# Seven half-size products for the five dense projections, with operands built in place, and down-weight sums formed where they are used

## The chip, the cores and the metric

The kernel runs on one core of a Trainium2 chip. The engines are TensorE (PE in the profile, PEld for its weight loads), VectorE (DVE), ScalarE (ACT), GpSimd (POOL) and SyncE (SP), whose queue issues all of this kernel's DMAs. The metric is the device time of one execution in microseconds (us). A measurement of this kernel tells differences from about 0.2% on.

## The reference

One decoder block over 1024 tokens of width 1024, in float32. Two sequence mixers (an SSD branch and a gated-linear-attention branch) are merged, then comes attention over 256 memory tokens and a gated FFN of width 2816, each with RMSNorm and a residual add:

```python
y_ssd = ssd_mixer(z, xBC, dt_raw, ...)
y_gla = gla_mixer(q, k, v, r, a1, ...)
merged = sigmoid(g_ssd) * (y_ssd @ w_up_ssd) + sigmoid(g_gla) * (y_gla @ w_up_gla)
h = h + merged @ w_o
q = rmsnorm(h) @ w_xq                 # 4 heads of 256
h = h + softmax(q k^T / 16) v @ w_xo  # k, v from the memory tokens
g, u = split(rmsnorm(h) @ w_ffn_in, 2)
h = h + (silu(g) * u) @ w_ffn_out
return rmsnorm(h)
```

The five matrices w_up_ssd, w_up_gla, w_o, w_xq and w_xo are 1024x1024 each; they are what the change is about, beside w_ffn_out.

## The kernel before

Activations are held transposed (features on partitions, tokens along the row) in quadrants: feature half i, token half j. Every float32 matrix product is made of three passes on parts of reduced precision: an operand is **split** into a high part, a copy on ACT (line 220), and a low part, a subtraction on DVE or POOL (line 74 records all calls of these two engines; the function `either` chooses one of them while the program is traced, by a running estimate of when each would be done). High x high, high x low and low x high are summed in PSUM.

The input projection, FFN-in and FFN-down use a scheme of seven products (Strassen's, in Winograd's form) in place of eight: with operand quadrants A (weights) and X, the products named B11, B21, T1, B22, T2, T3 and T4 use A11, A12, A21, A22 and sums of them (T1: A21+A22; T2: that less A11; B22: A12 less that; T3: A11-A21), and the same for X. The class `Operands` builds the X side, `Unit` the weight side for 256 columns, and `group` steps through the products, in the order SPACED for one unit and PAIRED for two.

The five dense projections before the change use plain products instead: `dense` walks over 8 blocks of 128 output features and 2 token halves, and each of these 16 outputs takes 24 matmuls of 128x128 by 128x512 into one PSUM bank (tiles `acc`), with weights split by `Left` (tiles `wd`, from `raw`) and inputs held split whole (tiles `hl`). After each output `post` evacuates the bank: sigmoid gates and a multiply for the two merges (the first one's result goes to DRAM, `ysg_d`, and comes back), a residual add, a store and a square for the statistics (`ssum`) of w_o and w_xo, a split for w_xq. Beside the first four of them runs `presum`: it loads w_ffn_out, forms the four sums that FFN-down's seven products need (tiles `sa` and `raw`) and stores them in DRAM (`down_d`).

Attention (`Att`) comes between w_xq and w_xo, head by head. FFN-in runs 11 pairs of units (gate and up), FFN-down (`stream`, `piece`, `fevac`) walks through 7 products of 11 rows of blocks, two at a time (a piece, 24 matmuls), and loads each piece's left and right operand from DRAM (tiles `fr`), splits them (tiles `fs`) and multiplies.

The order of instructions is set by a scheduler that takes the traced instructions by priority (`ahead` raises one); the engines run their queues in that order. Buffers come from pools: `op` 14 buffers of 8 KB per partition, `aux` 4, `m` 4; PSUM has 4 banks `acc` and 4 banks `bank`.

Of the kernel before, what the change touches and what calls it, by code (L numbers as in the profile page):

```python
# [9 lines left out]
F32 = mybir.dt.float32  # L10
# [6 lines left out]
P = 128  # L17
# [23 lines left out]
PAIRED = ("B11", "T1", "B21", "T2", "T3", "B22", "T4")  # L41
# [38 lines left out]
def block_kernel(ctx: ExitStack, tc: tile.TileContext, t: dict, out: bass.AP):  # L80
# [39 lines left out]
    down_d = dram("down_d", 4 * D_FF // 2, HALF)  # L120
# [105 lines left out]
    class Operands:  # L226
# [44 lines left out]
    class Unit:  # L271
# [18 lines left out]
        def left(s, name):  # L290
# [3 lines left out]
            if name == "T1":  # L294
                s.S, s.two = sums[s.side].tile([P, s.kh, P], F32, name="sa", tag="sa", bufs=2), False
# [9 lines left out]
            return {"B11": A11, "B21": A12, "B22": A12, "T3": A21, "T4": A22}.get(name, s.S)  # L305
# [83 lines left out]
    def group(units, B, then=(), nxt=None, frm=6, products=7):  # L389
# [6 lines left out]
        for n, name in enumerate((PAIRED if many > 1 else SPACED)[:products]):  # L396
# [692 lines left out]
    ysg_d = dram("ysg_d", D, TOK)  # L1089

    def load_blocks(src, row0, n, key="m"):
        r = []
        for k in range(n // 2):
            b = slot(key, name="in")
            SP.dma_start(b, src[row0 + 2 * k * P:row0 + (2 * k + 2) * P, :].rearrange("(i p) s -> p i s", p=P))
            r.append(b)
# [511 lines left out]
```

## Time and profile before

| what | value |
| --- | --- |
| three runs, us | 2013.74, 2016.06 (median), 2016.79 |
| profiled execution: time, us | 2017.15 |
| profiled execution: span, us | 2015.4 |
| mean granted clock of TensorE | 0.991 |
| instructions in the profile | 26277 |
| DMA traffic | 309.60 MB, mean 154 GB/s |

The span runs from the first to the last instruction that the profiler saw; the profiled execution's time is 1.75 us longer and lies 1.09 us above the median. The profile's lines have a source line, an engine, an operation, the tiles written and read, the shape, a count, the busy time and the mean time of one.

### The profile page before, as it was taken

To read this page: it belongs to the slowest core of one execution; us is meant where nothing else is said; L and a number is where in the kernel's file an instruction comes from. 1 tells how busy PE (TensorE), PEld (TensorE's weight loads), DVE (VectorE), ACT (ScalarE), POOL (GpSimd) and SP (SyncE) were. 2 spreads that over 40 slices of the span, in tenths; PEclk is the share of its full clock that TensorE was granted. 3 is DMA by queue.
4 is the path that set the end of the run, shared out by engine and by line. 5 is a ranking of instruction groups with operands and counts; after the bars stand their busy time and mean duration, and the time that the engine had idled before them with its cause. 6 is when DMAs were issued, how large, how long until landed. Compare 5 with 4: busy or idle time off the path is not lost.

```text
span 2015.4 us, 26277 instructions
## 1 busy us (share of the span) xinstructions
PE 1937.9 (96%) x9740; PEld 1617.2 (80%) x9740; DVE 1250.2 (62%) x1763; ACT 897.0 (45%) x1581; POOL 716.9 (36%) x524
## 2 busy tenths in 40 slices
PE   7798899999999999999999999998999999999998
PEld 6797687777777878888878888876888888888887
DVE  5855649879876655633444328566767667674465
ACT  7433844466553555542333226453343343354243
POOL 2612435556554212232134310244454554430002
PEclk9899999999999999999999999999999999999999
DMA  8441332255643755685775520432323323276463
GB/s 286 147 126 62 120 105 106 104 185 184 202 152 115 224 169 157 221 301 193 247 243 188 177 84 22 136 121 89 104 79 110 126 78 105 89 256 228 149 227 127
DMA packets 243365, 309.60 MB, mean 154 GB/s; under 512 B 14986, under 2 KB 162676, under 8 KB 243236
## 3 DMA queue, kind: packets, MB, share of 16 engines
q1 hardware_dynamic: 243236, 307.92, 45.6%
q8 instruction: 76, 1.25, 0.3%
q14 instruction: 53, 0.43, 0.1%
HBM read 211.07 MB, written 96.80 MB: 153 GB/s over the span
## 4 chain that ended last, share of the span: by engine, by line
PE 66%; DVE 8%; DMA 8%; POOL 6%; issue 6%; ACT 4%; SPq 2%; POOLq 0%; ACTq 0%; DVEq 0%
PE acc L52 58%; PE bank L52 7%; POOL raw L74 2%; DVE wlo L74 2%; DVE cv L74 1%; DMA raw<-in_w_in_dram 1%; PE bank L56 1%; POOL sa L74 1%; POOL y L74 1%; ACT whi L220 1%; DVE o L74 1%; DMA sr<-sr_d 1%; DMA vraw<-in_w_in_dram 1%; DMA ga<-yg_d 1%; ACT e L881 1%
## 5 line engine op out<-in xcount | busy, mean ns | idle before, releaser
L52 PE MATMUL acc<-hl,wd 128*128 128x512 f32 x1920 | 439.9, 390 | 1.7 <-DVE hl L74 0.8
L52 PEld LDWEIGHTS acc<-hl,wd 128*128 128x128 f32 x1920 | 360.1, 188 | 77.0 <-DVE hl L74 1.2
L74 DVE TENSOR_TENSOR wlo<-raw,whi 128x512 fp32r<-128x512 f32 x268 | 244.5, 915 | 129.4 <-ACT whi L220 128.7
L220 ACT ACTIVATE whi<-raw 128x512 fp32r<-128x512 f32 x272 | 169.8, 628 | 247.3 <-PE acc L52 194.7
L74 DVE TENSOR_TENSOR o<-acc,o 128x512 f32<-128x512 f32 (+1 forms) x160 | 107.2, 674 | 88.5 <-PE acc L52 85.9
L52 PE MATMUL acc<-fs 128*128 128x512 f32 (+1 forms) x792 | 156.2, 356 | 0.6 <-ACT o L1505 0.5
L74 POOL TENSOR_TENSOR sa<-raw 128x512 f32<-128x512 f32 x56 | 82.6, 1474 | 206.8 <-DMA raw<-in_w_ffn_out_dram 95.2
L52 PEld LDWEIGHTS acc<-fs 128*128 128x128 f32 x792 | 130.7, 189 | 21.6 <-ACT o L1505 0.9
L74 POOL TENSOR_TENSOR sa<-sa,raw 128x512 f32<-128x512 f32 x48 | 73.0, 1521 | 172.0 <-DVE wlo L74 172.0
L220 ACT ACTIVATE fs<-fr 128x1024 fp32r<-128x1024 f32 (+1 forms) x84 | 80.1, 984 | 110.2 <-PE acc L52 43.4
L74 DVE TENSOR_TENSOR fs<-fr,fs 128x1024 fp32r<-128x1024 f32 (+1 forms) x84 | 98.0, 1198 | 39.7 <-ACT fs L220 39.4
L74 POOL TENSOR_TENSOR raw<-raw,sa 128x512 f32<-128x512 f32 x48 | 76.8, 1600 | 91.6 <-DVE wlo L74 91.4
L220 ACT ACTIVATE whi<-sa 128x512 fp32r<-128x512 f32 x96 | 60.4, 629 | 109.2 <-PE acc L52 67.1
L74 POOL TENSOR_TENSOR raw<-raw 128x512 f32<-128x512 f32 x68 | 103.6, 1529 | 7.6 <-DVE sa L74 4.8
L74 DVE TENSOR_TENSOR wlo<-sa,whi 128x512 fp32r<-128x512 f32 x96 | 79.1, 824 | 37.7 <-ACT whi L220 37.5
L74 DVE TENSOR_TENSOR wd<-raw,wd 128x1024 fp32r<-128x1024 f32 x40 | 51.8, 1302 | 65.2 <-ACT wd L220 57.5
L74 DVE TENSOR_TENSOR ga<-acc,ga 128x512 f32<-128x512 f32 x64 | 43.8, 687 | 69.7 <-PE acc L52 56.0
L74 POOL TENSOR_TENSOR o<-o 128x512 f32<-128x512 f32 x39 | 63.4, 1629 | 59.4 <-DVE o L74 34.9
L52 PE MATMUL acc<-B22h,whi 128*128 128x512 f32 x192 | 77.4, 403 | 7.0 <-ACT whi L220 7.0
L52 PE MATMUL acc<-T2h,whi 128*128 128x512 f32 x192 | 77.4, 403 | 3.1 <-ACT whi L220 2.8
L52 PE MATMUL acc<-T2h,wlo 128*128 128x512 f32 x192 | 76.5, 399 | 3.8 <-DVE wlo L74 3.8
L52 PE MATMUL acc<-T1h,whi 128*128 128x512 f32 x192 | 76.2, 397 | 3.8 <-ACT whi L220 3.8
(370 smaller groups left out, 4832.9 us busy)
## 6 DMA issues: line engine op xcount, KB each, us to landing
raw<-in_w_in_dram SPq DMA_DIRECT2D x26, 1024.0 KB, 6.2
raw<-in_w_ffn_in_dram SPq DMA_DIRECT2D x22, 1024.0 KB, 7.6
act_d<-o SPq DMA_DIRECT2D x77, 256.0 KB, 2.0
fr<-act_d SPq DMA_DIRECT2D x35, 512.0 KB, 4.9
raw<-in_w_ffn_out_dram SPq DMA_DIRECT2D x11, 1024.0 KB, 6.9
fr<-down_d SPq DMA_DIRECT2D x20, 512.0 KB, 4.9
down_d<-raw SPq DMA_DIRECT2D x33, 256.0 KB, 2.7
raw<-in_w_xkv_dram SPq DMA_DIRECT2D x8, 1024.0 KB, 10.9
```

Of the source, the lines that this page charges most:

```text
L52: return s.e.matmul(o, x, y, **kw)
L56: return s.e.transpose(o, x, i)
L74: return f(*a, **kw)
L220: ACT.activation(hi, src, AF.Copy)
L881: ACT.activation(s.e[:, h], s.csb[:, h], AF.Relu, bias=cs[:, s.i0 + h:s.i0 + h + 1], scale=-1.0)
```

## The change

The five dense projections become products of seven as well (class `Product`), with whole quadrants of 512x512x512 each, every one in two halves of the inner dimension (24 matmuls each, 128x512). A `Grid` holds the four quadrants of an input as float32 tiles (`X`). `build(t)` forms the operands of half product t: it sums the weights in place in `raw`, splits them, sums the X quadrants in place, splits them, and puts the parts in two tiles `lr`; the loop builds two half products ahead (DEPTH). The products come in the order LATE. Each keeps four PSUM banks, one per 128 output features; `first` takes a bank's value into the output quadrant, `last` adds the bank to it and applies gate, residual or split. Gates and residuals are loaded by `early` into the rings `whi` and `wlo`. The first merge's result stays on the chip (`y_ys`), so `ysg_d` goes. Attention's heads come in another order, and two half products of w_xo are put into its end.

`presum` and `down_d` go. FFN-down's `stream` loads the raw quadrants of w_ffn_out (two for T1, B22 and T3, none for T2) and forms the sums there, with the running sum kept in tiles `rs`. `Unit.left` writes B22's left operand into the sum's tile instead of over A12, and two units are stepped in the order LATE instead of PAIRED.

```diff
-PAIRED = ("B11", "T1", "B21", "T2", "T3", "B22", "T4")
+LATE = ("B11", "T1", "T2", "B22", "T3", "B21", "T4")
@@ Unit.left
-            elif name in ("B22", "T2"):
-                if not s.two:
-                    sub(e, s.S, s.S, A11)
-                    s.two = True
-                if name == "B22":
-                    sub(either(A11, 2.0), A12, A12, s.S)
+            elif name == "T2":
+                sub(e, s.S, s.S, A11)
+            elif name == "B22":
+                sub(e, s.S, A12, s.S)
...
+    class Product:
+        RAW = {"B11": ((0, 0),), "T1": ((1, 0), (1, 1)), "B22": ((0, 1),), "T4": ((1, 1),)}
...
+        def left(s, name, ks):
+            r = lambda i, j: s.raw[i, j][:, ks]
+            e = lambda ap: either(ap, 2.0)
+            if name == "T1":
+                if ks.start == 0:
+                    s.S = s.raw[1, 1]
+                S = s.S[:, ks]
+                add(e(S), S, r(1, 0), S)
+                sub(e(S), r(1, 0), r(0, 0), r(1, 0))
+                return S
+            if name == "T2":
+                S = s.S[:, ks]
+                sub(e(S), S, S, r(0, 0))
+                return S
+            if name == "B22":
+                S = s.S[:, ks]
+                sub(e(S), S, r(0, 1), S)
+                return S
+            return r(*{"B11": (0, 0), "T3": (1, 0), "B21": (0, 1), "T4": (1, 1)}[name])
+
+        def build(s, t):
...
+            x = [slot("op", (P, 2, 2, HALF), F32R, name="lr") for _ in range(2)]
+            with ahead():
+                src = s.left(name, ks)
+                split(src, x[0][:, 0], x[0][:, 1], either(src))
+                if comb:
+                    comb[0](either(src, 1.0), q(of), q(comb[1]), q(comb[2]))
+                split(q(of), x[1][:, 0], x[1][:, 1], either(src))
+            s.hl[t] = x
+
+        def mm(s, t):
...
+            for k in range(2):
+                for u in range(4):
+                    for m, (a, b) in enumerate(((0, 0), (0, 1), (1, 0))):
+                        PE.matmul(s.p[u], w[:, a, k, u * P:(u + 1) * P], x[:, b, k],
...
+    DEPTH = 2
+    for t_ in range(4 * 14):
+        st, n = divmod(t_, 14)
+        nxt, m = divmod(t_ + DEPTH, 14)
+        if nxt < 4:
+            prods[nxt].build(m)
...
+        prods[st].mm(n)
...
@@ attention
+        if n >= 5:
+            if n < 9:
+                xo.build(n - 5)
...
+            if n in (7, 8):
+                xo.mm(n - 7)
@@ FFN-down, stream
-    LEFT = {"B11": (0, 0), "B21": (0, 1), "T1": 0, "B22": 3, "T2": 1, "T3": 2, "T4": (1, 1)}
+    LEFT = {"B11": ((0, 0),), "B21": ((0, 1),), "T1": ((1, 0), (1, 1)), "B22": ((0, 0), (0, 1)), "T2": (),
+            "T3": ((0, 0), (1, 0)), "T4": ((1, 1),)}
...
+                if name == "T1":
+                    add(e(), S, other, main)
+                elif name == "B22":
+                    sub(e(), S, S, other)
+                    sub(e(), main, main, S)
+                elif name == "T3":
+                    sub(e(), main, other, main)
+                split(S if name in ("T1", "T2") else main, x[0][:, 0], x[0][:, 1])
+                split(r[0][:, 1], x[1][:, 0], x[1][:, 1])
```

What this moves on the engines is shown at three places. First POOL in the product with w_up_gla. Before, where it ends the splits of inputs and works on the down weights' sums (`sa`, and `raw` of w_ffn_out):

```order
L74 TENSOR_TENSOR hl<-ga,hl 128x512 x15
L74 TENSOR_TENSOR raw<-raw 128x512 x2
L74 TENSOR_TENSOR hl<-ga,hl 128x512 x6
L74 TENSOR_TENSOR sa<-raw 128x512
L74 TENSOR_TENSOR raw<-sa,raw 128x512
```

After, in the same product, where `raw` holds quadrants of w_up_gla, `X<-X 128x1024` are sums of its input's quadrants, and `X` with `wlo` or `whi` are products with gates:

```order
L74 TENSOR_TENSOR raw<-raw 128x1024 x2
L74 TENSOR_TENSOR X<-X 128x1024
L74 TENSOR_TENSOR raw<-raw 128x1024
L74 TENSOR_TENSOR X<-X 128x1024
L74 TENSOR_TENSOR raw<-raw 128x1024 x4
L74 TENSOR_TENSOR X<-X 128x1024
L74 TENSOR_TENSOR X<-X,wlo 128x512
L74 TENSOR_TENSOR X<-X,whi 128x512
```

The 128x512 sums for a later stage have left, and 128x1024 sums that this product's own matmuls need stand there now.

Second DVE in the same product. Before, per output one add or product from PSUM (`ga<-acc,ga`), a sum and a low part, and a weight block's low part (`wd`) for every two outputs:

```order
L74 TENSOR_TENSOR ga<-acc,ga 128x512 x3
L74 TENSOR_TENSOR ga<-ga 128x512
L74 TENSOR_TENSOR hl<-ga,hl 128x512
L74 TENSOR_TENSOR ga<-acc,ga 128x512
L74 TENSOR_TENSOR ga<-ga 128x512
L74 TENSOR_TENSOR wd<-raw,wd 128x1024 x2
```

After, from the last evacuations of w_up_ssd (`X<-bank`) into T1 and T2 of w_up_gla:

```order
L74 TENSOR_TENSOR lr<-X,lr 128x1024
L74 TENSOR_TENSOR raw<-raw 128x1024
L74 TENSOR_TENSOR X<-bank,wlo 128x512
L74 TENSOR_TENSOR X<-bank,whi 128x512
L74 TENSOR_TENSOR lr<-raw,lr 128x1024
L74 TENSOR_TENSOR X<-bank,wlo 128x512
L74 TENSOR_TENSOR X<-bank,whi 128x512
L74 TENSOR_TENSOR lr<-X,lr 128x1024
L74 TENSOR_TENSOR lr<-raw,lr 128x1024
L74 TENSOR_TENSOR X<-X 128x1024
```

Two low parts of 128x1024 per half product stand among the evacuations, some behind sums that POOL forms.

Third POOL at the change from FFN-in to FFN-down. Before, where the last sums of FFN-in are followed by a few residual and statistics adds (`ssum`):

```order
L74 TENSOR_TENSOR sa<-sa,raw 128x512
L74 TENSOR_TENSOR o<-o,ssum 128x512
L74 TENSOR_TENSOR raw<-raw,sa 128x4x128
L74 TENSOR_TENSOR o<-o 128x512 x5
L74 TENSOR_TENSOR o<-o,ga 128x512
L74 TENSOR_TENSOR ssum<-ssum,sq 128x512 x6
```

After, at the same place (`rs` is the running sum of w_ffn_out's quadrants):

```order
L74 TENSOR_TENSOR o<-o 128x512 x5
L74 TENSOR_TENSOR rs<-fr 128x1024 x5
L74 TENSOR_TENSOR rs<-fr 128x512
L74 TENSOR_TENSOR rs<-rs,fr 128x1024 x2
L74 TENSOR_TENSOR fr<-fr,rs 128x1024
L74 TENSOR_TENSOR rs<-rs,fr 128x1024 x3
L74 TENSOR_TENSOR rs<-rs,fr 128x512
L74 TENSOR_TENSOR fr<-fr,rs 128x512
L74 TENSOR_TENSOR o<-o,ga 128x512
L74 TENSOR_TENSOR fr<-fr 128x1024 x5
```

The sums of T1, B22 and T3 stand there now, one or two per piece; four of B22's second sums are on DVE (`fr<-fr,rs`).

More of the change, by code (lines that the diff above doesn't have):

```diff
@@ L395, in group @@
         many = len(units)
[L396 removed]
+        for n, name in enumerate((LATE if many > 1 else SPACED)[:products]):
             for x, u in enumerate(units):
@@ L1136, in block_kernel @@
-    left = Left((t["w_up_ssd"], t["w_up_gla"], t["w_o"], t["w_xq"], t["w_xo"]))
-    def paired(keys):
-        return [(lambda k=k: slot(k, (P, 2, TOK), F32R, name="hl")) for k in keys]
-    def hl(slots_, k):
-        if callable(slots_[k]):
-            slots_[k] = slots_[k]()
-        return slots_[k]
-    def into(slots_, k, j, src, e=None):
-        x = hl(slots_, k)
-        split(src, x[:, 0, half(j)], x[:, 1, half(j)], e)
-    def dense(no, ins, post, pre=lambda o, j: None, js=JS):
-        todo = [(o, j) for o in range(NB) for j in js]
-        nxt = pre(*todo[0])
-        for n, (o, j) in enumerate(todo):
-            w = left[NB * no + o]
-            cur, nxt = nxt, pre(*todo[n + 1]) if n + 1 < len(todo) else None
-            p = acc()
-            m = 0
-            for k in range(NB):
-                for a, b in ((0, 0), (0, 1), (1, 0)):
-                    PE.matmul(p, w[:, a, k], ins[k][:, b, half(j)], start=m == 0, stop=m == 3 * NB - 1)
-                    m += 1
-            with ahead():
-                post(o, j, p, cur)
-            yield
@@ new lines, in residual, with first, last, last_xq @@
+    def residual(got, to, store, stats, gain):
+        def first(o, j, p):
+            add(DVE, to(o, j), p, got.pop((o, j)))
+        def last(o, j, p, alone):
+            h = ga()
+            add(DVE, h, p, got.pop((o, j)) if alone else to(o, j))
+            SP.dma_start(store[o * P:(o + 1) * P, half(j)], h)
+            ACT.activation(to(o, j), h, AF.Copy, scale=col(gain, o))
+            stats.take(j, h)
+        return first, last
+    s1 = Stats(rp)
+    i_q = {}
+    def last_xq(o, j, p, alone):
+        if (o // 2, j) not in i_q:
+            i_q[o // 2, j] = slot("op", (P, 2, 2, HALF), F32R, name="qhl")
+        x = i_q[o // 2, j]
+        if alone:
+            return split(p, x[:, 0, o % 2], x[:, 1, o % 2], DVE)
+        q = x_o(o, j)
+        add(DVE, q, p, q)
+        split(q, x[:, 0, o % 2], x[:, 1, o % 2], either(q))
@@ L1395, in block_kernel @@
         gu.append([gate, up])
[L1396 to L1406 removed]
+    B = Operands(x_ffn, 4, order=LATE)
+    for n in range(2, 14):
+        if n + DEPTH < 14:
+            xo.build(n + DEPTH)
+            if n % 2 == 0 and n // 2 + 2 < 7:
+                xo.load(n // 2 + 2)
+        xo.mm(n)
+        if n == 9:
             gu[0][0].load()
[L1408 removed]
+        elif n == 11:
             gu[0][1].load()
+        elif n >= 12:
+            B.upto(4 * (n - 11))
     def ffn_side():
         for _ in range(2):
+            yield
+        u_xo_stats.close(1)
+        yield
+        u_xo_stats.rows(1)
+        lag[0] = 1
+        for _ in range(3):
             yield
```

319 lines of the change are left out of this document (161 added, 158 removed).

## The prediction

> **What bounds the kernel now.** I read the busy shares of the page first, then the chain that ended last, then busy time by stretches (start:end and length in us, then busy us and instruction count of PE, PEld, DVE, ACT and POOL, the granted clock, the DMA share and GB/s).
>
> ```profile
> PE 1937.9 (96%) x9740; PEld 1617.2 (80%) x9740; DVE 1250.2 (62%) x1763; ACT 897.0 (45%) x1581; POOL 716.9 (36%) x524
> PE 66%; DVE 8%; DMA 8%; POOL 6%; issue 6%; ACT 4%; SPq 2%; POOLq 0%; ACTq 0%; DVEq 0%
> 847.00:937.00 90.00, 89.81 (x396) 74.10 (x395) 33.02 (x42) 36.19 (x55) 27.32 (x20) 1.00 0.81 277
> 937.00:1030.00 93.00, 93.00 (x412) 77.03 (x412) 43.14 (x54) 26.67 (x40) 19.29 (x14) 1.00 0.68 231
> 1030.00:1120.00 90.00, 88.53 (x390) 72.77 (x389) 39.67 (x43) 28.20 (x41) 41.32 (x29) 1.00 0.62 208
> 1120.00:1208.00 88.00, 88.00 (x398) 73.16 (x397) 23.19 (x30) 18.08 (x28) 13.92 (x12) 1.00 0.35 123
> 1208.00:1283.00 75.00, 73.54 (x444) 64.71 (x443) 49.64 (x122) 42.67 (x107) 0.00 (x0) 1.00 0.10 32
> 1475.00:1627.40 152.40, 152.40 (x674) 126.17 (x673) 106.10 (x124) 60.22 (x104) 79.24 (x52) 1.00 0.31 104
> 1830.00:1900.00 70.00, 70.00 (x310) 58.03 (x309) 36.95 (x41) 27.54 (x31) 0.00 (x0) 1.00 0.61 207
> ```
>
> TensorE is full almost everywhere. The first four of these stretches are the dense products with w_up_ssd, w_up_gla, w_o and w_xq, the fifth is attention, the sixth is FFN-in, the last a piece of FFN-down. In the dense products VectorE and GpSimd have room; in FFN-in they have little. From the timeline of PE, the pace and the limits of the dense stage:
>
> ```profile
> 834.78 0.39 PE L52 MATMUL acc<-T4h,whi 128*128 128x512 f32 x1
> ...
> 847.02 0.39 PE L52 MATMUL acc<-T2h,wlo 128*128 128x512 f32 x1
> 847.25 1.07 PE L52 MATMUL acc<-hl,wd 128*128 128x512 f32 x4
> ...
> 1207.96 5.91 PE L52 MATMUL acc<-kvhl,hl 128*128 128x256 f32 x48
> ```
>
> Between the first two rows lie 54 steps, so a 128x512 matmul costs 12.24 / 54 = 0.2267 us. The four dense products take 1207.96 - 847.25 = 360.7 us.
>
> Now the two engines that must feed a product of seven. Timelines of DVE alone, of DVE and POOL together, groups by form, and the dense stage's groups:
>
> ```profile
> 1040.43 1.22 DVE L74 TENSOR_TENSOR wd<-raw,wd 128x1024 fp32r<-128x1024 f32 x1 [5.29 <-ACT wd L220]
> 1041.57 0.68 DVE L74 TENSOR_TENSOR hl<-ga,hl 128x512 fp32r<-128x512 f32 x1
> 1042.17 0.68 DVE L74 TENSOR_TENSOR ga<-acc,ga 128x512 f32<-128x512 f32 x1
> ...
> 1347.87 4.09 DVE L74 TENSOR_TENSOR T2l<-o,T2h 128x512 fp32r<-128x512 f32 x3
> 1351.89 0.68 DVE L74 TENSOR_TENSOR o<-o 128x512 f32<-128x512 f32 x1
> ...
> 1348.03 1.69 POOL L74 TENSOR_TENSOR sa<-sa,raw 128x512 f32<-128x512 f32 x1 [0.63 <-DVE wlo L74]
> 1349.67 1.74 POOL L74 TENSOR_TENSOR o<-o 128x512 f32<-128x512 f32 x1
> ...
> L74 POOL TENSOR_TENSOR vraw<-vraw 128x1056 f32<-128x1056 f32 x2 | 4.9, 2436 | 0.0
> L74 POOL TENSOR_TENSOR sa<-raw 128x512 f32<-128x512 f32 x9 | 11.6, 1289 | 122.9 <-DMA raw<-in_w_ffn_out_dram 95.2 <-DVE ga L74 23.4 <-DVE hl L74 4.3
> L74 DVE TENSOR_TENSOR ga<-acc,ga 128x512 f32<-128x512 f32 x48 | 32.8, 687 | 56.3 <-PE acc L52 45.2 <-ACT ga L1220 6.1 <-issue 3.0
> L220 ACT ACTIVATE wd<-raw 128x1024 fp32r<-128x1024 f32 x40 | 41.9, 1055 | 53.0 <-DMA down_d<-raw 31.3 <-PE acc L52 18.3 <-DMA raw<-in_w_up_ssd_dram 2.5
> ```
>
> Starts of successive rows give DVE 1.14 us for 128x1024 and 0.60 for 128x512. GpSimd takes 1.29 for 128x512 (1.27 taken, for back-to-back work) and 2.44 for 128x1056, so about 2.4 for 128x1024. The middle rows decide the forecast: three DVE subtractions, worth 3 x 0.60 = 1.8, took 4.09 while two POOL operations ran beside them, and the POOL operations took 1.69 and 1.74 in place of 1.29. The sum, 1.8 + 2 x 1.27 = 4.3, is what both took together. **Two-input SBUF work of VectorE and GpSimd runs one after the other**, not side by side. An operation that reads PSUM is spared: ga<-acc,ga keeps 0.687 on average in stretches where POOL works. I call the shared resource the port.
>
> How full can the port be with TensorE still full? In FFN-in, 1475 to 1627.4, the row above has 124 DVE and 52 POOL operations, almost all 128x512, and of DVE's these read PSUM:
>
> ```profile
> L74 DVE TENSOR_TENSOR o<-acc,o 128x512 f32<-128x512 f32 x24 | 16.5, 689 | 16.7 <-PE acc L52 15.5 <-DMA act_d<-o 1.1
> ```
>
> The other 100 at 0.60 and POOL's 52 at 1.27 make 126 of 152.4 us, 83%; with the 24 that read PSUM 140, 92%. TensorE was busy for 152.40 of 152.40. So a port load of 83% is hidden there. A load above 100% cannot be.
>
> **The change, part by part.** *Matmuls.* Each dense product had 16 x 24 = 384 matmuls and gets 7 x 48 = 336. Five times 48 at 0.2267 is 54.4 us less: 43.5 in the first four products, 10.9 in w_xo. TensorE alone would need 360.7 - 43.5 = 317.2 for the four.
>
> *Building operands.* Counts are from the program's order. Per product, 28 subtractions make low parts (128x1024), 8 sums form left operands in place and 8 form right ones. The five products together put 154 of these on DVE and 66 on POOL. With the evacuations' SBUF steps the port carries, at 1.14, 0.60, 2.4 and 1.27:
> w_up_ssd: DVE 33 wide and 3 narrow, POOL 11 and 9: 37.6 + 1.8 + 26.4 + 11.4 = 77.2.
> w_up_gla: 31 and 13, 13 and 15: 35.3 + 7.8 + 31.2 + 19.1 = 93.4.
> w_o: 30 and 6, 14 and 8: 34.2 + 3.6 + 33.6 + 10.2 = 81.6.
> w_xq: 31 and 6, 13 and 6: 35.3 + 3.6 + 31.2 + 7.6 = 77.7.
> That is 329.9 us against 4 x 336 x 0.2267 = 304.7 of matmuls: 101, 123, 107 and 102% of a product's 76.2 us. Besides, 76 operations read PSUM on DVE, 45.6 us at 0.60. The port is the new bound, and two half products of lead (10.9 us) can't smooth what every product exceeds. Floor: 330 us, if each PSUM read lies beside a POOL operation. Ceiling: 330 + 45.6 + 10 = 386, if none does and a chain of POOL sum, ACT copy and DVE subtraction (2.4 + 1.06 + 1.14 = 4.6) shows by about half once per product. POOL holds 171 of the 330, so half of the PSUM reads find it beside them: 330 + 23 + 10 = 363, and I take that. Against 360.7 it is **+2**; the ends are -31 and +25. What lies behind TensorE's wait is more of its own product only: nothing else stands in its queue, so no later work fills the gap.
>
> *ACT.* 28 copies at 1.055 and some 28 evacuations and gates at about 0.6 are 46 of 76 us: hidden.
>
> *Removed.* The presums of the down weights, their 22 MB of traffic and 44 sums, the ysg_d round trip and the split of inputs go. They were hidden under a full TensorE in the first four stretches, so they are worth nothing beyond the port's time, which is counted anew above. The five 1 MB weight loads per product in place of four go where the DMA share was 0.81 at most, and 22 MB of presum traffic has left: 0. On SP's queue the gates' and residuals' loads now go into the two rings of three that hold FFN weights' parts, four per step, so two of four wait for an evacuation of the step before; behind them wait the next weight's loads, which have a whole step (10.9 us) in hand: 0, or part of the slow rival below.
>
> *Attention, w_xo, start of FFN-in.* The waits of PE from 1300 to 1450 (engine, waited for, us, times, longest):
>
> ```profile
> PE acc L52 <- ACT whi L220: 3.7, 5, 1.3
> PE bank L52 <- DVE ssum L74: 2.2, 1, 2.2
> PE acc L52 <- DVE wlo L74: 2.0, 3, 1.5
> ```
>
> These 7.9 us are operands of FFN-in that come late. Gain: 10.9 of matmuls and, since two halves of w_xo are put into attention's end, its 75.00 - 73.54 = 1.5 of idle time. POOL is idle in attention (0.00), so four of 14 builds hide there. Behind it remain 59 us of w_xo's port work, 36 of FFN operands (26 low parts and 3 sums on DVE, 2 and 13 on POOL) and 19 of the first pair's weights, 114; half of 34 PSUM reads adds 10. TensorE has 12 x 5.44 + 38.1 = 103.4 for it. 21 us stick out, 16 after one half product of lead, where 7.9 were lost before: +8. Net **-4**, ends -12 (all hidden) and +7 (PSUM reads all serial).
>
> *FFN-down.* 1830:1900 shows POOL 0.00 and DVE 36.95 of 70, so sums fit on average. In B22 each piece of 24 matmuls (5.44 us) needs two low parts and two sums; with five whole pieces and a half one that is 11 low parts and 4 sums on DVE at 1.14, and 5.5 + 1.5 sums on POOL at 2.4: 12.5 + 4.6 + 16.8 = 33.9. Four residual adds (2.4) and half of T1's four PSUM reads (1.2) make 37.5 against 132 x 0.2267 = 29.9. T1 and T3 need 12.5 + 13.2 = 25.7 and stay under it. Less a part of the lead that is **+6**, ends 0 and +16. Transfers grow from 1 to 1.5 MB per piece: 207 GB/s becomes 289 at most at 0.61 x 289 / 207 = 0.85 of the engines, and 277 was reached at 0.81. That is inside the upper end.
>
> *Order LATE, the left sum of B22 written to sa.* The same four sums per unit in another order: 0.
>
> Sum: +2 - 4 + 6 = +4 against the profiled execution's 2017.15 (span 2015.4), which stands 1.1 above the median, 2016.06. On the median: 2020 to 2021; I say 2021.
>
> **Rivals.** *TensorE stays the bound* (faster). It needs DVE and POOL to work side by side on these wide operations: DVE's own 54 us and POOL's 51 in w_up_gla are both under 76. Then 54.4 + 1.5 go: 2016 - 56 = 1960. Against it stand the serial rows. [...] Chance 0.12.
> *The port bounds, but its PSUM reads hide and lead covers the rest* (faster): 330 for four products, -31, with -12 and 0 behind: 1973 to 2000. It decides once less than half of the PSUM reads are serial and no bubbles show. FFN-in's full TensorE at 92% with every PSUM read counted speaks for it. Chance 0.18.
> *The in-order queues lose more than the port* (slower): a DVE row that waits for ACT behind a POOL sum keeps PSUM evacuations and low parts behind it waiting, while POOL has nothing it may overwrite. +25, +7 and +16 give 2041 to 2064. Chance 0.20.
> The Trainium skill, page SBUF — State Buffer, section SBUF: two separate sides, calls the shared pair an exclusive lock that is held for the whole instruction, by GpSimd or by a VectorE operation with two SBUF inputs. The trace agrees (4.09 us for three operations). By this rule a 128x1024 sum on POOL shuts VectorE out for its whole length, which no row here shows for a full dense stage; the first rival would need it to fail.
>
> **How the numbers follow.** The forecast, 2001 to 2041, has 0.50. The range leaves out the first rival and the upper half of the last, 0.12 + 0.08: 1973 to 2058. A measurement can tell 0.2%, 4 us. Below 2012 lie 0.12, 0.18 and 0.13 of the forecast's case: faster 0.43. Same 0.11. Slower 0.20 and 0.26: 0.46.
>
> **What the profile after would show.** Right: TensorE under 90% busy in the four products, waits on DVE lr and ACT lr, most in w_up_gla and at T1 of each product; DVE lr<-raw,lr well above its 1.2 us on average and POOL raw<-raw above 2.4; lr matmuls 1680; the four products near 360 us, FFN-down with small waits in B22. Wrong: TensorE at 99% in them, or DVE's mean for lr at 1.2 while POOL is as busy; or FFN-down or the start of FFN-in long by 20 us or more.

## The result, and the profile after

The changed kernel takes 2074.98 us in the median (2072.50 to 2087.46), the kernel before 2014.9 beside it: a ratio of 1.0315, with a 95% interval of 1.0277 to 1.0353. It is slower by 60 us, where 2021 was predicted with a range up to 2058. The profiled execution took 2087.46, 12.5 above its median, which the stage times below carry with them.

Page of the changed kernel: span, busy time of each engine, and the chain that ended last.

```profile
span 2085.7 us, 25828 instructions
PE 1917.9 (92%) x9500; PEld 1592.5 (76%) x9500; DVE 1494.3 (72%) x1846; ACT 986.7 (47%) x1669; POOL 933.6 (45%) x581
PE 54%; DVE 19%; DMA 9%; ACT 7%; POOL 6%; issue 5%; SPq 1%; POOLq 0%; DVEq 0%; ACTq 0%
```

TensorE has 240 matmuls less, as foreseen, and is still busy for only 20 us less. At 0.2267 us each the 240 are worth 54.4, so 1937.9 should have become 1883.5; the 34.4 us above that are matmuls that ran slower (mean granted clock 0.967, before 0.991). By stages, 14.1 of them fall in the four products (321.7 busy, where 351.1 - 43.5 = 307.6 was due; granted clock 0.95, before 1.00), 7.4 in attention and w_xo (0.94, before 1.00) and 8.1 in FFN-down (0.93, before 0.99). Its idle time rose from 2015.4 - 1937.9 = 77.5 to 2085.7 - 1917.9 = 167.8. The balance is -54.4 + 34.4 + 90.3 = +70.3, the difference of the two spans.

Where it went shows in TensorE's timeline, by the first matmul of each stage: the dense products (`lr`), attention (`kvhl`), FFN-in (`B11h`), FFN-down (`fs`).

```profile
866.10 11.04 PE L52 MATMUL bank<-lr 128*128 128x512 f32 x48
...
1227.10 5.08 PE L52 MATMUL acc<-kvhl,qhl 128*128 128x256 f32 x41
...
1382.47 0.77 PE L52 MATMUL acc<-B11h,whi 128*128 128x512 f32 x1 [7.30 <-DVE ga L74]
...
1818.80 0.39 PE L52 MATMUL acc<-fs 128*128 128x512 f32 x1
```

The same starts in the kernel before are 847.25, 1207.96, 1349.48 and 1779.32. The first of them was misread in the prediction. In the kernel before, matmuls of the group ahead still stand between the first dense ones; its timeline:

```profile
851.82 0.39 PE L52 MATMUL acc<-B22h,whi 128*128 128x512 f32 x1
...
863.83 0.39 PE L52 MATMUL acc<-T4h,wlo 128*128 128x512 f32 x1
```

There are 36 of them from the first row to the last, 8.2 us. So the four products took 360.7 - 8.2 = 352.5, and they began, in effect, at 855.4. The stages, in us, from one profiled execution each (the experiments' rows are discussed below):

| kernel | start of dense stage | four products | attention and w_xo | FFN-in | FFN-down | span |
| --- | --- | --- | --- | --- | --- | --- |
| before | 855.4 | 352.5 | 141.5 | 429.8 | 236.1 | 2015.4 |
| changed | 866.1 | 361.0 | 155.4 | 436.3 | 266.9 | 2085.7 |
| e1_left | 860.7 | 350.2 | 141.5 | 430.8 | 235.5 | 2018.6 |
| e2_down | 855.4 | 350.5 | 141.5 | 430.2 | 266.7 | 2044.3 |
| e3_dve_prod | 861.0 | 328.0 | 145.4 | 436.2 | 263.3 | 2034.0 |
| e4_banks | 862.3 | 358.6 | 152.5 | 436.6 | 244.0 | 2054.1 |
| e10_fixed_t3 | 854.1 | 321.5 | 144.2 | 436.4 | 238.8 | 1995.0 |
| e11_junk | 862.8 | 411.3 | 168.5 | 437.5 | 264.1 | 2144.2 |
| e12_ffn_dve | 852.6 | 323.3 | 141.4 | 435.9 | 241.7 | 1994.9 |

(In e1_left and e2_down, too, the 36 matmuls are taken off.) The changed kernel loses in every stage: 10.7 before the dense stage, 8.5 in the four products, 13.9 in attention and w_xo, 6.5 in FFN-in, 30.8 in FFN-down. Kernels e3_dve_prod and e4_banks are equal to the changed one up to the dense stage and start it 4 to 5 us earlier, so that much of the 10.7 is put down to this one execution, not to the change.

In the four products TensorE keeps its pace but for the beginning of each. A step of 48 matmuls at full pace takes 10.88 us; timeline of the first two products:

```profile
881.70 2.07 PE L52 MATMUL acc<-lr 128*128 128x512 f32 x4 [4.56 <-ACT lr L219]
888.62 12.57 PE L52 MATMUL acc<-lr 128*128 128x512 f32 x44 [4.84 <-DVE lr L74]
...
911.91 11.04 PE L52 MATMUL acc<-lr 128*128 128x512 f32 x48
922.79 11.04 PE L52 MATMUL bank<-lr 128*128 128x512 f32 x48
933.67 11.04 PE L52 MATMUL acc<-lr 128*128 128x512 f32 x48
944.55 11.04 PE L52 MATMUL bank<-lr 128*128 128x512 f32 x48
955.43 11.04 PE L52 MATMUL acc<-lr 128*128 128x512 f32 x48
966.31 0.39 PE L52 MATMUL bank<-lr 128*128 128x512 f32 x1
967.66 5.75 PE L52 MATMUL bank<-lr 128*128 128x512 f32 x24 [0.97 <-DVE lr L74]
975.47 7.08 PE L52 MATMUL bank<-lr 128*128 128x512 f32 x23 [2.05 <-DVE lr L74]
982.39 11.04 PE L52 MATMUL acc<-lr 128*128 128x512 f32 x48
```

The T1 steps of the four products took 19.3, 16.1, 20.4 and 21.0 us, the B11 steps 15.6, 10.9, 14.4 and 17.7; the others lost 1 to 2 us at most. TensorE is busy for 321.7 of the 361.0 us, 89%; VectorE's low parts take 1.64 us (from `raw`) and 1.90 (from `X`) on average and GpSimd's sums of `raw` 2.98, as the prediction said of the port. What stands on VectorE and GpSimd in the T1 step of w_up_gla, from their timelines:

```profile
967.53 3.43 DVE L74 TENSOR_TENSOR lr<-raw,lr 128x1024 fp32r<-128x1024 f32 x1
970.88 1.21 DVE L74 TENSOR_TENSOR X<-X 128x1024 f32<-128x1024 f32 x1
972.02 3.40 DVE L74 TENSOR_TENSOR lr<-X,lr 128x1024 fp32r<-128x1024 f32 x1
975.34 1.21 DVE L74 TENSOR_TENSOR lr<-raw,lr 128x1024 fp32r<-128x1024 f32 x1
...
966.48 3.40 POOL L74 TENSOR_TENSOR raw<-raw 128x1024 f32<-128x1024 f32 x1
971.04 3.29 POOL L74 TENSOR_TENSOR raw<-raw 128x1024 f32<-128x1024 f32 x1 [1.16 <-DVE lr L74]
```

A row of 3.4 us on the one engine spans the other's operation and its own: 3.40 on DVE from 972.02 is POOL's sum up to 974.33 and then 1.1 us of its own. The two alternate.

### The profile page after: what moved, and what is told of

Same layout as the page of the kernel before. It is cut to its first block, busy times and chain, and to the rows that moved or that the text cites. A ratio compares the mean times of both kernels' runs of the same rounds, so it can differ in the third digit from the quotient of the medians.

```text
span 2085.7 us, 25828 instructions
## 1 busy us (share of the span) xinstructions
PE 1917.9 (92%) x9500; PEld 1592.5 (76%) x9500; DVE 1494.3 (72%) x1846; ACT 986.7 (47%) x1669; POOL 933.6 (45%) x581
## 4 chain that ended last, share of the span: by engine, by line
PE 54%; DVE 19%; DMA 9%; ACT 7%; POOL 6%; issue 5%; SPq 1%; POOLq 0%; DVEq 0%; ACTq 0%
PE acc L52 43%; PE bank L52 9%; DVE lr L74 5%; DVE X L74 3%; DVE cv L74 2%; DVE wlo L74 2%; DMA raw<-in_w_in_dram 1%; POOL X L74 1%; DMA fr<-in_w_ffn_out_dram 1%; PE bank L56 1%; DMA csb<-cs_d 1%; POOL raw L74 1%; ACT lr L219 1%; DVE raw L74 1%; DMA fr<-act_d 1%
## 5 line engine op out<-in xcount | busy, mean ns | idle before, releaser
L52 PE MATMUL acc<-lr 128*128 128x512 f32 x864 | 209.1, 400 | 24.0 <-DVE lr L74 14.6
L52 PEld LDWEIGHTS acc<-lr 128*128 128x128 f32 x864 | 165.9, 193 | 62.9 <-DVE lr L74 17.2
L52 PE MATMUL bank<-lr 128*128 128x512 f32 x816 | 196.0, 399 | 18.8 <-DVE lr L74 10.7
L52 PEld LDWEIGHTS bank<-lr 128*128 128x128 f32 x816 | 156.3, 193 | 55.7 <-DVE lr L74 13.6
L74 POOL TENSOR_TENSOR raw<-raw 128x512 f32<-128x512 f32 (+1 forms) x79 | 159.7, 2025 | 43.6 <-DVE lr L74 32.4
L74 POOL TENSOR_TENSOR X<-X 128x1024 f32<-128x1024 f32 (+1 forms) x39 | 98.1, 2530 | 58.7 <-DVE lr L74 39.3
L74 DVE TENSOR_TENSOR lr<-raw,lr 128x1024 fp32r<-128x1024 f32 x66 | 109.3, 1656 | 18.0 <-ACT lr L219 18.0
L74 DVE TENSOR_TENSOR lr<-X,lr 128x1024 fp32r<-128x1024 f32 x62 | 114.1, 1843 | 10.5 <-ACT lr L219 10.5
L219 ACT ACTIVATE lr<-raw 128x1024 fp32r<-128x1024 f32 x70 | 73.8, 1054 | 74.3 <-POOL raw L74 43.0
L74 POOL TENSOR_TENSOR sa<-raw,sa 128x512 f32<-128x512 f32 x48 | 75.1, 1564 | 70.1 <-DVE wlo L74 70.1
## 6 DMA issues: line engine op xcount, KB each, us to landing
raw<-in_w_xkv_dram SPq DMA_DIRECT2D x8, 1024.0 KB, 10.9
```

Source lines behind the costliest of these rows:

```text
L52: return s.e.matmul(o, x, y, **kw)
L74: return f(*a, **kw)
L219: ACT.activation(hi, src, AF.Copy)
```

## Experiments

Each ratio is against the kernel before, run on the same chip.

**e1_left**, the kernel before with this alone:

```diff
...
-            elif name in ("B22", "T2"):
-                if not s.two:
-                    sub(e, s.S, s.S, A11)
-                    s.two = True
-                if name == "B22":
-                    sub(either(A11, 2.0), A12, A12, s.S)
+            elif name == "T2":
+                sub(e, s.S, s.S, A11)
+            elif name == "B22":
+                sub(e, s.S, A12, s.S)
...
```

> The kernel before with one part of the change alone: B22's left operand is written into the sum's tile instead of over A12. Theory 1: since A12 is no longer overwritten, this sum need not wait for B21's split and goes earlier on GpSimd, beside the convolution's VectorE work, so that a low part comes late once per unit (wait on DVE wlo 1.3 us in the changed kernel). Then this part alone costs the 10 us by which the changed kernel enters the dense stage late: about 2025 against 2015. Theory 2: the place of the sum is free and the 10 us come from later work that the scheduler pulled forward: 2015, within 3.

Measured: 2022.26, ratio 1.0032 (1.0020 to 1.0045). The place of the sum costs about 6 us, 5.3 of them ahead of the dense stage: theory 1 in kind, at about half its size (the rest is put down to the one execution). TensorE's waits from 300 to 420 us, where convolution runs beside the units, first of the kernel before, then of e1_left:

```profile
PE acc L52 <- ACT whi L220: 3.3, 6, 0.6
...
PE acc L52 <- DVE wlo L74: 8.0, 6, 1.3
```

Six units, six waits, 0.8 us more each. GpSimd's timeline has B22's sum, again of the kernel before and then of e1_left:

```profile
343.68 2.80 POOL L74 TENSOR_TENSOR raw<-raw,sa 128x512 f32<-128x512 f32 x1 [4.82 <-DVE wlo L74]
...
341.34 2.27 POOL L74 TENSOR_TENSOR sa<-raw,sa 128x512 f32<-128x512 f32 x1 [1.75 <-DVE wlo L74]
```

The old sum waits 4.8 us, for B21's low part to have read A12; the new one only for T2's, and runs beside VectorE's convolution, which it delays, and with it the next low part.

**e2_down**, the kernel before with FFN-down's `stream` of the changed one; `presum` and `down_d` are gone:

```diff
...
-    early = presum()
+    early = iter(())
...
-    LEFT = {"B11": (0, 0), "B21": (0, 1), "T1": 0, "B22": 3, "T2": 1, "T3": 2, "T4": (1, 1)}
+    LEFT = {"B11": ((0, 0),), "B21": ((0, 1),), "T1": ((1, 0), (1, 1)), "B22": ((0, 0), (0, 1)), "T2": (),
+            "T3": ((0, 0), (1, 0)), "T4": ((1, 1),)}
...
```

> The kernel before with FFN-down's sums formed in FFN-down and the presums with their DRAM traffic taken out; the dense projections stay plain. Theory 1: FFN-down's loss is its own (T1's evacuations stand on VectorE behind B22's operands, which wait for loads and GpSimd sums), so it takes 249 instead of 218 us behind the last act_d store and the total is about 2046; the removed presums give nothing back in the dense stage. Theory 2 (as predicted): the sums are hidden but for B22, +6, 2021. Theory 3: the lost time came from late work of the dense stage and FFN-in, and FFN-down alone costs nothing: 2015 or less.

Measured: 2045.04, ratio 1.0139 (1.0109 to 1.0168). Theory 1: FFN-down takes 266.7 us, as in the changed kernel (266.9), behind dense products that are the old ones. The removed presums, 44 sums and 22 MB, give back 2 us at most (350.5 against 352.5, one execution each).

**e3_dve_prod**, the changed kernel with `Product`'s operands on VectorE:

```diff
-            e = lambda ap: either(ap, 2.0)
+            e = lambda ap: DVE
...
-                split(src, x[0][:, 0], x[0][:, 1], either(src))
+                split(src, x[0][:, 0], x[0][:, 1], DVE)
...
-                    comb[0](either(src, 1.0), q(of), q(comb[1]), q(comb[2]))
+                    comb[0](DVE, q(of), q(comb[1]), q(comb[2]))
...
-                split(q(of), x[1][:, 0], x[1][:, 1], either(src))
+                split(q(of), x[1][:, 0], x[1][:, 1], DVE)
```

> The changed kernel with all sums and low parts of class Product on VectorE; GpSimd keeps only the gates' products and adds. Theory 1 (shared port): a T1 step issues six sums and four low parts. With the sums on GpSimd that is 6 x 2.4 + 4 x 1.14 = 19.0 us one after the other (measured steps 19.3, 16.1, 20.4, 21.0); all on VectorE it is 10 x 1.14 = 11.4, about a step of matmuls (10.9). The four products go from 361 to 315-325 us, the whole to about 2030, VectorE's means fall to 1.2 us. Theory 2 (side by side, GpSimd's own chain of six sums, 14.4 us, is the limit of T1): 3 us per product, 2063. Theory 3 (chains of sum, ACT copy and low part in in-order queues, whatever the engine): T1 stays near 16, 2060 or more.

Measured: 2034.78, ratio 1.0093 (1.0069 to 1.0116); four products 328.0, a little above theory 1's 315 to 325. All of `Product`'s operand work was given to one engine and the kernel became 40 us faster: theory 1. VectorE's means stay at 1.3 us, not 1.2, where GpSimd still has the gates. In w_up_gla no step is longer than 10.9 any more.

**e11_junk**, e3_dve_prod with GpSimd work that nobody needs:

```diff
                 split(q(of), x[1][:, 0], x[1][:, 1], DVE)
+                if jk[0] is not None:
+                    for k in range(2):
+                        nc.gpsimd.tensor_tensor(jk[0], x[0][:, 0, k], x[1][:, 0, k], ALU.add)
...
+    jk[0] = rp.tile([P, HALF], F32, name="jk", tag="jk", bufs=1)
```

> The port by itself: the kernel with Product on VectorE, and for each half product two sums of 128x512 of the high parts on GpSimd into a tile that nobody reads, 28 per product, some 108 in the four products and 28 in w_xo. GpSimd would be busy for about half of the stage, and nothing waits for these sums but the release of the operand tiles. Theory 1 (shared port): 35.6 us more per product on loads of 63, 77, 64 and 61 make 99, 113, 100 and 97 us against 76.2 of matmuls: the four products go from 328 to 400-420 us, the whole from 2035 to 2110-2140, and VectorE's 128x1024 means rise from 1.2 to about 2. Theory 2 (side by side): the four products stay near 328, the whole near 2035, VectorE's means stay 1.2.

Measured: 2146.19, ratio 1.0646 (1.0626 to 1.0666), 6 us above theory 1's range; four products 411.3, inside it; attention and w_xo 168.5. Groups by form, low parts, an evacuation and the added sums, first of e3_dve_prod, then of e11_junk:

```profile
L74 DVE TENSOR_TENSOR lr<-raw,lr 128x1024 fp32r<-128x1024 f32 x70 | 91.5, 1308 | 13.3 <-ACT lr L219 13.1
L74 DVE TENSOR_TENSOR X<-bank,X 128x512 f32<-128x512 f32 x20 | 13.0, 682 | 5.6 <-PE bank L52 5.5
...
L1179 POOL TENSOR_TENSOR jk<-lr 128x512 f32<-128x512 f32 x136 | 282.5, 2077 | 178.4 <-ACT lr L219 170.9
L74 DVE TENSOR_TENSOR lr<-raw,lr 128x1024 fp32r<-128x1024 f32 x70 | 133.3, 1905 | 2.4 <-ACT lr L219 2.1
L74 DVE TENSOR_TENSOR X<-bank,X 128x512 f32<-128x512 f32 x20 | 12.7, 675 | 0.0
```

This is the port by itself. 108 sums of 1.27 us (137 us) into a tile that nobody reads lengthen the four products by 83. The low parts' mean goes from 1.31 to 1.91 us, with no more idle time ahead of them; the same engine's adds that read PSUM keep their 0.68. VectorE is busy for 392.5 of the 411.3 us (287.8 of 328.0 without these sums), so it was not kept waiting until GpSimd had released the operand tiles. Side by side it would have stayed near 328.

**e4_banks**, the changed kernel with fresh banks for B22 of FFN-down:

```diff
-        p = bank()
+        p = acc()
...
             elif name == "T1":
                 add(DVE, q(1, 1), p, q(1, 0))
+            elif name == "B22":
+                add(DVE, q(0, 1), p, q(1, 1))
                 later(1, 1, fold)
-            elif name == "B22":
-                add(DVE, q(0, 1), p, q(1, 0))
...
-        if name in ("B11", "T1", "T2") and k == 0:
-            banks = [(bank if name == "T1" else acc)() for _ in range(4)]
-        fresh = name in ("B11", "T1", "T2")
+        fresh = name in ("B11", "T1", "B22", "T2")
+        if fresh and k == 0:
+            banks = [(bank if name in ("T1", "T2") else acc)() for _ in range(4)]
```

> The changed kernel with other PSUM banks for B22 of FFN-down: B22 starts fresh in the four acc banks and its evacuation adds T1's result from SBUF; T2 to T4 use the bank tiles. B22's matmuls then need not wait for T1's evacuations. Theory 1 (queue order): the wait of 14.3 us goes, with 2 to 3 us of matmuls at half clock behind it: about 2058 against 2075. Theory 2 (supply): B22's operands come no faster than loads and sums allow, and the wait only moves to DVE fs or ACT fs: 2070 or more.

Measured: 2056.10, ratio 1.0195 (1.0168 to 1.0221); FFN-down 244.0 instead of 266.9. Timelines of the changed kernel, TensorE with T1 and B22, then VectorE between them:

```profile
1885.35 30.08 PE L52 MATMUL bank<-fs 128*128 128x512 f32 x132
1929.76 30.62 PE L52 MATMUL bank<-fs 128*128 128x512 f32 x124 [14.32 <-DVE o L74]
...
1900.52 1.23 DVE L74 TENSOR_TENSOR fr<-fr,rs 128x1024 f32<-128x1024 f32 x1 [3.66 <-DMA fr<-in_w_ffn_out_dram]
1902.92 4.56 DVE L74 TENSOR_TENSOR fs<-fr,fs 128x1024 fp32r<-128x1024 f32 x2 [1.18 <-ACT fs L219]
1910.86 3.46 DVE L74 TENSOR_TENSOR fs<-fr,fs 128x1024 fp32r<-128x1024 f32 x2 [3.39 <-ACT fs L219]
...
1926.72 2.29 DVE L74 TENSOR_TENSOR fr<-fr,rs 128x1024 f32<-128x1024 f32 x1
1928.93 0.68 DVE L74 TENSOR_TENSOR o<-bank,o 128x512 f32<-128x512 f32 x1
```

T1's matmuls end at 1915.43. Its evacuation, 0.68 us, starts at 1928.93, because VectorE's queue has sums and low parts for B22 in front of it and these wait for loads and GpSimd. B22 adds to the same banks and stands still for 14.3 us. In e4_banks, B22 starts at once:

```profile
1876.18 30.08 PE L52 MATMUL bank<-fs 128*128 128x512 f32 x132
1906.10 16.71 PE L52 MATMUL acc<-fs 128*128 128x512 f32 x73
1923.65 13.67 PE L52 MATMUL acc<-fs 128*128 128x512 f32 x59 [0.85 <-DVE fs L74]
```

B22's operands came in time but for 0.85 us: theory 1. Supply was not the limit; the order on one queue was, together with banks that B22 had to share with T1. Later in FFN-down TensorE still waits 5.9 us for evacuations (8.7 in the changed kernel).

**e5_combo**, e3_dve_prod's and e4_banks' edits, the old `Unit.left`, and FFN-down's sums on VectorE:

```diff
...
-                e = lambda: either(main, 2.0)
+                e = lambda: DVE
```

> The changed kernel with four edits together: the old left operand of B22 in units (over A12), class Product's sums and low parts on VectorE, the other PSUM banks for B22 of FFN-down, and FFN-down's left sums on VectorE. If the losses are separate, their sizes from single edits add: 2035 (Product on VectorE) less 5 to 6 (left operand), less 19 to 23 (banks), less 0 to 6 (sums of FFN-down, 2 x 1.14 + 2 x 1.14 = 4.6 us per B22 piece of 5.44): 2000 to 2010, the first version under the kernel before's 2015. Rival: VectorE becomes the bound in FFN-down (in B22 25 us of operands, 4.8 of evacuations and residuals for 29.9 of matmuls), FFN-down stays above 250 and the whole above 2013.

Measured: 2001.35, ratio 0.9926 (0.9912 to 0.9941). This lies at the low end of the sum: the losses are separate, and the rival falls (FFN-down 239.8). The fourth edit, FFN-down's sums on VectorE, was not measured alone. In FFN-in's first pair this kernel forms B21 from the quadrant that B22's sum has already overwritten, since that pair runs in the order LATE; its output is thus not the reference's. **e9_fixed** is the same work made whole:

```diff
...
-                sub(e, s.S, A12, s.S)
+                o = s.S if s.late else A12
+                sub(e, o, A12, s.S)
+                return o
...
```

> The four edits together (Product on VectorE, the other PSUM banks for B22 of FFN-down, FFN-down's sums on VectorE, old left operand of B22), with the old left operand in single units alone; the first pair of FFN-in, whose order has B21 after B22, keeps the new one, so that the whole computation is that of the reference. The timed work is the same as with the four edits: 2001 within 3, against 2015 of the kernel before and 2075 of the changed one. Rival: the first pair's other left operand costs what FFN-in's start lost, 4 us: 2005.

Measured: 2004.42, ratio 0.9947 (0.9930 to 0.9963), between the two expectations, and the medians can't tell them apart. The traces speak for the rival: FFN-in takes 436.2 us against e5_combo's 432.6, and TensorE waits 5.5 us for the first pair's B22 operand, a wait that e5_combo hasn't.

**e6_t3late**, the changed kernel with one sum moved from T1's operands to T3's:

```diff
-                sub(e(S), r(1, 0), r(0, 0), r(1, 0))
...
+            if name == "T3":
+                sub(e(S0 := r(1, 0)), S0, r(0, 0), S0)
```

> The changed kernel with one sum of class Product formed later: A11 - A21 with T3's operands instead of with T1's. The sums per product, their engines' choice and the shared port are the same. Theory 1 (bursts against the lead): operands can be built at most two half products ahead, so T1's and T2's sums, 33.2 us of port work, have 27.2 us, and 6 us per product stick out; with the sum in T3 it is 28.4 us in 27.2, and 52.0 in 49.0 to T3's end, 3 stick out: 3 us less per product, 12 to 15 in all, 2060 to 2063, with T1's steps near 15. Theory 2 (sum over a product, as predicted): the port's work per product is what counts, 2075 within 5.

Measured: 2071.93, ratio 1.0278 (1.0260 to 1.0297); T1's steps 17.1, 17.2, 20.8, 22.7. This looks like theory 2, but the edit moved nothing to T3: nothing held the sum back, so the scheduler still put it ahead of T2's sums. It also put all 32 sums of `raw` in the four products on GpSimd, where VectorE had formed 7 of them. The run decides nothing.

**e7_combo_t3** adds the same edit and later loads to e5_combo (with the same overwritten quadrant in the first pair):

```diff
-        if st == 0 and n in (2, 5, 8, 10):
+        if st == 0 and n in (5, 7, 9, 11):
```

> The four edits together, with A11 - A21 formed with T3, and the loads of w_up_gla's input quadrants put three to one steps later, since in the run with Product on VectorE they stand ahead of w_up_ssd's T1 weights on SP's queue (9.5 us for two of them, waiting for stores). Left in that run are 9.6 us of waits in w_up_ssd, 9.2 in w_o, 4.4 in w_xq. Theory: T1 loses 2.3 us of sums on VectorE and w_up_ssd's weights come earlier: 6 to 12 us less than the four edits alone. Rival: what is left hangs on the last outputs of the product before (a data dependence), and nothing changes, within 3.

Measured: 2003.86, ratio 0.9941 (0.9925 to 0.9958), which can't be told from e5_combo. In w_o's T1 the sums of `raw` stand on VectorE in the same places as in e5_combo: here too nothing held the moved one back.

**e10_fixed_t3** makes the move binding, on e9_fixed, and has e7_combo_t3's later loads:

```diff
-                sub(e(S), r(1, 0), r(0, 0), r(1, 0))
...
+            if name == "T3":
+                sub(e(r(0, 0)), r(0, 0), r(0, 0), r(1, 0))
-            return r(*{"B11": (0, 0), "T3": (1, 0), "B21": (0, 1), "T4": (1, 1)}[name])
+            return r(*{"B11": (0, 0), "T3": (0, 0), "B21": (0, 1), "T4": (1, 1)}[name])
...
```

> The version with the four edits made whole, and A11 - A21 written over A11 instead of over A21, which T2's sum reads before; so the scheduler cannot form it ahead of T2's sums, as it did when it was only written down later. w_up_gla's input loads stand one to three steps later. Theory 1 (bursts at the start of a product): T1 has 2.3 us less of VectorE work in w_o, w_xq and w_up_ssd, where T1 or B11 still lose 4 to 9 us: 5 to 8 us less than without these edits, 1993 to 1996. Theory 2 (what is left at the start of a product waits for the last outputs of the product before): no change, within 2.

Measured: 1999.18, ratio 0.9924 (0.9906 to 0.9943); four products 321.5 where e9_fixed has 329.0. The T1 steps of w_up_ssd, w_o and w_xq went from 16.1 to 13.8, from 18.1 to 16.7 and from 15.2 to 10.9 us. The burst at a product's start counts, as theory 1 said, with 5.2 us less in all (the two intervals overlap; the steps are from one execution each); but 6 us remain at w_o's T1, whose input is the product before's output. Of the 7.5 us at most 1.6 come from the later loads (e7_combo_t3's four products, with the loads and without a real move, took 327.1 against e5_combo's 328.7).

**e8_combo_paired**, e5_combo with FFN-in's first pair in the old order:

```diff
-        for n, name in enumerate((LATE if many > 1 else SPACED)[:products]):
+        for n, name in enumerate((PAIRED if many > 1 else SPACED)[:products]):
...
-    B = Operands(x_ffn, 4, order=LATE)
+    B = Operands(x_ffn, 4, order=PAIRED)
```

The scales of token half 0 are formed after the first gates use them, so its values are not the reference's.

> The four edits together, with the first pair of FFN-in in the old order (B11, T1, B21, T2, T3, B22, T4). Theory: B21 needs no sum, and between T1 and T2 it spreads the operand work at the start of FFN-in, where the changed kernel waits 5.6 us for diag behind sums and low parts: 3 to 6 us less than the four edits alone. Rival: B21's right operand is the quadrant that w_xo ends with, so it comes late and TensorE waits: 2 to 5 us more.

Measured: 2014.25, ratio 0.9989 (0.9970 to 1.0007), 13 us more than e5_combo, and neither story fits: TensorE's longest wait there was 9.5 us for T2's left low part (DVE wlo), not for B21's operand. Why that part came late stays open.

**e12_ffn_dve**, e10_fixed_t3 with FFN-in's shared operand on VectorE:

```diff
...
-    B = Operands(x_ffn, 4, order=LATE)
+    B = Operands(x_ffn, 4, order=LATE, only=DVE)
```

> The fastest version so far (1999) with the right sums and right low parts of FFN-in's shared operand on VectorE too. In that version 13 sums of 128x512 on GpSimd (mean 1.61 us) stand at the start of FFN-in, where TensorE still waits 4.5 us for evacuations, 3.3 for diag and 5.5 for a left operand. Theory (port): 13 x (1.27 - 0.60) = 8.7 us less port work there, the start of FFN-in gets 5 to 8 us shorter, 1991 to 1994. Rival (queue order): the evacuations and diag stand behind still more VectorE work, which takes the gain back: 1997 or more.

Measured: 1995.85, ratio 0.9897 (0.9880 to 0.9913), the fastest version: 1% under the kernel before, 79 us under the changed one. Its interval overlaps that of e10_fixed_t3 (0.9924), so the last edit's own gain is not certain; attention and w_xo take 2.8 us less, and FFN-down, which the edit does not touch, 2.9 more. The predicted 5 to 8 did not come. At FFN-in's start the wait for evacuations fell to 3.3 us, those for diag (a small VectorE product by which TensorE spreads a norm's scales) rose from 3.3 to 6.8, which is what the rival said of diag.

## Why the prediction was wrong

The sum was +4 and came to +60 in the medians, +70 between the two profiled executions. FFN-down is 24.8 us of that error, attention with w_xo and FFN-in 24.4, the stretch before the dense stage 10.7 (put at 0), the four products 6.5. The four products, on which the forecast was built, are thus the smallest part. The terms that failed most, FFN-down and attention with the start of FFN-in, added up how much work sticks out, while what counted was which operation stands in front of which on an engine's queue; this is shown for FFN-down (e4_banks) and only in part for the other.

*Matmuls, -54.4.* The count was right. The price was not: the matmuls that are left ran 34.4 us longer. After its longer waits TensorE starts at about half pace; timeline of the changed kernel at the start of FFN-in:

```profile
1383.04 0.63 PE L52 MATMUL acc<-B11l,whi 128*128 128x512 f32 x1
1383.47 0.63 PE L52 MATMUL acc<-B11h,wlo 128*128 128x512 f32 x1
...
1387.73 0.63 PE L52 MATMUL acc<-B11h,whi 128*128 128x512 f32 x1
...
1389.00 0.39 PE L52 MATMUL acc<-B11l,whi 128*128 128x512 f32 x1
1389.22 0.39 PE L52 MATMUL acc<-B11h,wlo 128*128 128x512 f32 x1
```

Between the first and the third row lie 11 steps: 0.43 us each in place of 0.23. From 1382.47 to 1389.00, 16 steps take 6.5 us in place of 3.6, so the wait of 7.3 us costs some 3 us more. In e3_dve_prod the wait at this place is 2.5 us, and from the second matmul on the steps are 0.23. The prediction had no term for this.

*Building operands, the port, +2.* The mechanism was right and is shown: e3_dve_prod by taking GpSimd's share away, e11_junk by adding to it. The total, 363, was close too (361.0), in part by luck: the 33 us above 330 were costed as PSUM reads and as chains in every product, and came as waits at the products' starts with 14.1 us of slow matmuls behind them. Two more things in it were wrong. The baseline of 360.7 held 8.2 us of other work, so the term came to +8.5. And the account per product did not hold: w_up_gla, costed as the worst with 93.4, took 81.4 (955.43 to 1036.8), and w_up_ssd, costed at 77.2, took 89.3. w_up_gla's input lies in DRAM long before; the others' first operands wait for a load or for the outputs of the product before. So the work comes as a burst in B11 and T1, which the lead of two half products does not cover (e10_fixed_t3 shows it for 2.3 us of sums in T1; how much of the rest is a wait for loads or outputs was not separated).

*Attention, w_xo, start of FFN-in, -4.* Measured +13.9 and +6.5. (Its own numbers give ends of about -20, the 7.9 us lost before included, and +6, not -12 and +7.) The failing step is "four of 14 builds hide there" in attention, with "16 after one half product of lead" behind it: it counted what sticks out at the end and not what stands in front of whom. In attention a VectorE operation of 0.2 us, the softmax's scale (`mx`), stood behind w_xo's operands; timelines of VectorE and ACT in the changed kernel, then VectorE and TensorE in FFN-in's first pair:

```profile
1280.80 2.77 DVE L74 TENSOR_TENSOR X<-X 128x1024 f32<-128x1024 f32 x1
1283.50 0.68 DVE L74 TENSOR_REDUCE mx<-bank 128x2 f32<-128x512 f32 x1
1284.10 1.21 DVE L74 TENSOR_TENSOR X<-X 128x1024 f32<-128x1024 f32 x1
1285.23 0.22 DVE L74 SCALAR_TENSOR_TENSOR mx<-mx,xsc 128x2 f32<-128x2 f32 x2
...
1285.47 0.56 ACT L1361 ACTIVATE pe<-bank,mx,xsc 128x256 f32<-128x256 f32 x1 [10.41 <-DVE mx L74]
...
1378.31 3.42 DVE L74 TENSOR_TENSOR T1l<-X,T1h 128x512 fp32r<-128x512 f32 x2
1381.65 0.68 DVE L74 TENSOR_TENSOR ga<-acc,wlo 128x512 f32<-128x512 f32 x1
...
1416.42 0.79 PE L52 MATMUL acc<-B22h,whi 128*128 128x512 f32 x1 [3.72 <-ACT whi L219]
```

ACT waited 10.4 us for it, TensorE 5.7 for ACT. At FFN-in's start the same befell w_xo's last evacuations, behind `B11l`, `T1l` and `X<-X`: 7.3 us (the row at 1382.47). With less on the port the stage of attention and w_xo shrinks to 145.4 (e3_dve_prod) and 141.4 (e12_ffn_dve), so port and queue order share its +13.9; that the place in the queue alone did it was not tried. The +6.5 of FFN-in is another matter. It stays in every kernel that eases the port (435.9 to 436.6), and behind the first 48 us FFN-in runs without a wait. In e5_combo, which forms the first pair's B22 operand over A12, FFN-in takes 432.6. Written into the sum's tile, that operand can only be formed when T2's has been split, on GpSimd behind sums of `X`, and TensorE waits for it, 3.7 us in the changed kernel (the row at 1416.42) and 5.5 in e9_fixed.

*FFN-down, +6.* Measured +30.8, and e2_down shows it apart from all the rest. "Four residual adds and half of T1's four PSUM reads" were costed at 3.6 us of port time. What mattered was that T1's reads stand behind B22's operands while B22 needs their banks: 14.3 us, plus slow matmuls behind each wait. e4_banks takes away 22.9 of the 30.8, and the +7.9 that stays is near the term's +6, though with waits for evacuations (5.9 us), not for operands, in it. Transfers kept inside their bound: in e4_banks B22's operands come 0.85 us late, with the DMA share at 0.77 in T1 and 0.48 in B22.

*Order LATE and B22's left sum, 0.* Measured +6 (e1_left, for the left sum alone, in the old order), and the first pair's wait above, where the order LATE puts B22 right behind T2. "The same four sums per unit in another order" overlooked that writing elsewhere removes a dependence, and the scheduler then moves the sum beside other port work.

*Removed presums, 0.* Right within 2 us (e2_down).

*The rivals.* "TensorE stays the bound" is refuted by e11_junk. The second, in which the lead covers the rest, needed 330 us for the four products and fails by their 361.0. The third, in-order queues, had the right mechanism at three of the places, but the chances gave it 0.20, and its terms +25, +7 and +16 were in the wrong places: the four products needed less, the other two 20 and 31. Even its 2064 lies under the 2075. The signs named for a wrong forecast, FFN-down or the start of FFN-in long by 20 us or more, are what came. The Trainium skill, page SBUF — State Buffer, section SBUF: two separate sides, has GpSimd or a VectorE operation with two SBUF inputs lock the other out for the whole instruction; e11_junk agrees for a whole stage (means of 1.91 against 1.31 us), and operations that read PSUM were spared (0.675 against 0.682).

## What to carry to other kernels

Before moving element-wise work from VectorE to GpSimd "because it is idle", compare what each costs on the shared port: here 2.4 us on GpSimd against 1.14 on VectorE for a 128x1024 sum, so that giving all of `Product`'s operands to the busier engine saved 40 us. When operands are built inside a product, list for each short and urgent operation (an evacuation, a softmax scale, a diag) what may stand ahead of it in its engine's queue, and give banks to the next product that do not hang on the last one's evacuation. Take a stage's baseline from rows that hold this stage's work only, and add the slow matmuls behind each new wait of several us (some 3 us behind one of 7.3 here).

## What the hardware showed beyond expectation

GpSimd's sums of 128x512 beside a busy VectorE took 2.08 us on average (e11_junk) against 1.27 alone, and VectorE's low parts 1.91 against 1.31: for work with two inputs in SBUF nothing is gained by running both. Where the port's sum exceeds the matmuls, it is nearly the time: e3_dve_prod's two-input work comes to 266 us by the prices of the prediction, and with 108 sums of 1.27 to 403, where 411.3 was measured. Where it stays below, as in e3_dve_prod with 266 against 304.7 of matmuls, 23 us are still lost, most of them at the start of a product. And a wait has a tail: after the one of 7.3 us the matmuls ran at about half pace for 5.7 us (1382.47 to 1388.16).
